# Two blocks of attention layers on one core: scores of two row groups issued in turn into two banks, and weighted sums with the head loop innermost

## The chip, the core and the metric

The kernel runs on one core of a Trainium2 chip. The metric is the time on the device in microseconds (us). Three runs of the kernel before took 1917.32, 1917.56 and 1919.44 us; the median is 1917.56 us.

## The reference, cut to what matters

256 tokens of width 1024 pass two layers of a first block (feed-forward, mixer, feed-forward) and two layers of a second block. The change lies in the mixer of the first block, which has three attentions beside each other; the one it touches most is the forgetting attention, 8 heads of 64 channels:

```python
u = rmsnorm(h); q, k, v = heads(u @ w_in)         # 8 heads of 64, 256 tokens
c = cumsum(log_sigmoid(f_logit + b_forget))       # per head, over the tokens
z = q @ k.T * 64 ** -0.5 + c[:, None] - c[None, :]
o_fx = softmax(where(k_pos <= q_pos, z, -max)) @ v
o_sb = ...    # stick-breaking attention, 8 heads of 64: weights w from a cumulative sum, then w @ v
o_mem = ...   # 4 heads of 128 on a memory of 256 tokens
h = h + rmsnorm((g_sb * (o_sb @ w_sb) + g_fx * (o_fx @ w_fx) + g_mem * (o_mem @ w_mem)) @ w_out)
```

All is float32.

## The kernel before

**Main line and tasks.** TensorE runs strictly in the order in which the program emits it. Its main line is the products with the weights. A weight chunk of 128 x 1024 is loaded (`raw`), cast into a high part by ScalarE (`hi`, L270) and into a rest by VectorE (`lo`, L271), and each product is three matmuls, at L287, L288 and L290 for products with tokens in the rows (tiles `acc`, `gu`), and at L298 to L300 for those with channels in the rows (`mm`, `cf`). Eight `hi` and eight `lo` buffers exist, so a cast of a chunk waits until TensorE has finished the chunk eight places back. What hangs on other engines is emitted by tasks (Python generators). The program keeps a clock `now` of TensorE's work in ns: `tick(ns)` advances it, each product by its own columns, and a task that yields a number of ns (`DELAY`) goes on once `now` has advanced so far. So a smaller tick in a task puts more products of the main line between that task and what follows. The other engines' orders are made by a scheduler.

**The mixer** (`mixer`, L760) runs in this order: projections of queries and keys (`mm`), then the three gates (`acc`, 3 x 8 chunks, each chunk for token tile 0 and then for token tile 1), then three branch products, then the output product. Beside them the tasks put in the three attentions, one after the other.

**Forgetting attention** (`forgetting`, L666). A unit (`forgetting_unit`, L677) takes the scores of a token tile t of 128 queries: at t = 0 four heads with 128 keys each, at t = 1 two heads with 256 keys, so that a unit fills one bank of PSUM. Heads 4e+j lie at partitions 64e to 64e+63 of block j of q and k, so e says which half of the array's rows a head's score product uses, and all heads of a unit have the same e. There are two such banks (`z_bank`, bufs=2), used in turn. A layer has six units: t = 0 with e = 0 and 1, then t = 1 with e = 0 (two), e = 1 (two). A unit's scores (L684) are followed on VectorE by one add of the decay per head (L690) and a row maximum (L547), on ScalarE by one exponential per head (L551), which is the last reader of the bank. Units are `fox_gap` = 2000 ns and the unit's tick of 860 ns apart.

**Weighted sum** (`weighted`, L555): normalize (L560, L561), transpose p into a bank `tr` (L383; two such banks, in turn), copy it out (pT, L564), multiply with v (L570) into another `tr` bank, and split the result into `acth` (ScalarE, L375) and `actl` (VectorE, L376). For heads of 64 channels, head i goes to partitions 64 (i % 2) of the result, which is one half of the array's columns. The loop is head by head, and within a head over its key tiles. `stick_breaking_half` (L586) has the same kind of sum for its heads at L631, and `memory_unit` (L705) uses z banks and `weighted` with heads of 128.

In the page's forms, 64*128 is a matmul on 64 rows and 128 columns of the array, 128*64 one on 128 rows and 64 columns. Each float32 matmul of q, k, p and v is two instructions in the trace, so a unit's 4 matmuls at t = 0 are 8, and its 2 at t = 1 are 4.

Of the kernel before, what the change touches and what calls it, by code (L numbers as in the profile page):

```python
# [29 lines left out]
# ---------------------------------------------------------------- host layout  # L30
def _by_k(w):
    """[K, N] -> [K/128, 128, N]"""
    return w.reshape(w.shape[0] // P, P, w.shape[1])


def _by_col(w):
    """[K, n*128] -> [n, 128, (K/128)*128]: one chunk holds all of K for 128 columns."""
    k, n = w.shape[0] // P, w.shape[1] // P
    return w.reshape(k, P, n, P).transpose(2, 1, 0, 3).reshape(n, P, k * P)


def _side_by_side(parts):
    """[K, w] each -> [K/128, 128, sum of w]"""
    return _by_k(np.concatenate(parts, axis=1))


def _woven(parts):
    """[K, n*128] each -> chunks of 128 columns, in turn from each part"""
    return np.stack([_by_col(p) for p in parts], axis=1).reshape(-1, P, parts[0].shape[0])


def _pairs(a):
    """[n, 128, w] -> [n/2, 128, 2w]"""
    n, p, w = a.shape
    return a.reshape(n // 2, 2, p, w).transpose(0, 2, 1, 3).reshape(n // 2, p, 2 * w)


def _head_cols(w, first, width, stride, n):
    """Columns first..first+width of each of n heads, stride apart."""
# [3 lines left out]
def _halves(w):  # L63
    """Columns of eight heads of 64 in the order 0 4 1 5 2 6 3 7"""
# [10 lines left out]
def _three(w):  # L75
    """[8*128, 320] -> 3 chunks of three row tiles, the last one's third tile being zeros"""
# [20 lines left out]
def _per_partition(I):  # L97
    """Small per-channel vectors, channel c at partition c % 128."""
# [13 lines left out]
def _consts():  # L112
    """Constants of the shapes alone: masks, rotary tables."""
    i = np.arange(P)
    after = (i[:, None] > i[None, :])          # [k, k']: 1 where k > k'
    strict = (i[:, None] < i[None, :])         # [k, q]: 1 where k < q
    cmask = np.where(i[None, :] <= i[:, None], 0.0, NEG)   # [q, k]
# [11 lines left out]
# ---------------------------------------------------------------- program  # L129
class Act:  # L130
    """An operand [nk*128 channels, 256 tokens], channel-major, in a high and a low part; tiles of
    four channel blocks."""
# [12 lines left out]
    def part(self, k, n, t):  # L145
        """Blocks k..k+n of the tokens of tile t, both parts"""
# [12 lines left out]
class Program:  # L159
    """TensorE runs in the order of emission. The products with weights are its main line; what  # L160
    hangs on other engines' results (transposes, attention) is emitted by tasks, generators that
    yield how many ns of TensorE's work are to lie before their next step."""
# [8 lines left out]
                 decay=8000, fox_gap=2000, fox_p=13900, mem_gap=3000, mem_p=19500, mem_norm=17000, conv0=2200, conv_gap=3000,  # L171
# [17 lines left out]
    # -- tasks  # L189
# [44 lines left out]
    # -- tiles  # L234
# [18 lines left out]
    # -- inputs  # L253
# [7 lines left out]
    def take(self, src, i, parts=1):  # L261
        """Chunk i of a re-laid weight, split exactly into a high part and the rest."""
# [18 lines left out]
    # -- matrix products  # L281
    def mm_a(self, outs, x, k, t, hi, lo, first, last):
        """Token-major: outs += x[k, tokens of t].T @ chunk; outs: [(psum, columns of the chunk)]"""
# [9 lines left out]
    def mm_b(self, ps, x, hi, lo, nk, base=0):  # L293
        """Channel-major: ps[128 channels, 256 tokens] = sum over k of chunk[k].T @ x[k]"""
# [8 lines left out]
    def cols_b(self, src, blocks, x, nk, per, evac):  # L303
        """Blocks of 128 channels, `per` of them in a chunk; evac(block, psum [128, 2, 256]) for
        every two blocks."""
# [10 lines left out]
    def rows_a(self, chunks, outs, x, done, head=0, tail=0, ready=(None, None)):  # L316
        """Token-major products over all of K. chunks: functions that give a row tile's chunk;
        outs[t]: the accumulators; done(t) follows the last product of token tile t. The first
        `head` and the last `tail` row tiles go to one token tile after the other, so that what
        comes before or after on the other engines runs beside products; of the last ones, also  # L320
        one accumulator after the other. ready: the tasks that make x for each token tile."""
# [34 lines left out]
    def whole(self, src, nk, per=1, parts=1):  # L356
        """Row tiles, `per` of them in a chunk"""
# [10 lines left out]
    def banks(self, n, w=512):  # L368
        """Accumulators of n row products of width w for both token tiles, and their columns"""
# [3 lines left out]
    def split(self, dst, src, lo_engine=None):  # L373
        """dst[0] + dst[1] = src exactly"""
# [3 lines left out]
    def transposed(self, *parts):  # L378
        """[128, n*128] each -> psum [128, all blocks, 128]"""
# [11 lines left out]
    # -- norms  # L391
    def rstd(self, sums):
        """(sum of sums + eps)^-1/2, sums being shares of a mean of squares"""
# [9 lines left out]
    def mean_sq(self, src, scale):  # L403
        """The row sums of (scale * src)^2"""
# [16 lines left out]
    def gained(self, ps, g):  # L421
        """ps [128 channels, 4 blocks, 128] times the blocks' gains g [128, 4]"""
# [4 lines left out]
    def pre_gain(self, t, g, x, r, delay):  # L427
        """x[:, tokens of t] = h * g, transposed and split; the norm's factor r[:, t] is left to the
        products' results."""
# [12 lines left out]
    def pre_norm(self, t, g, x, delay, h=None):  # L442
        """x[:, tokens of t] = norm of h, transposed and split"""
# [7 lines left out]
    def residual(self, t, ps, post):  # L451
        """h += ps, or its norm with the gain `post`"""
# [15 lines left out]
    def across(self, r, ready):  # L468
        """r [128 tokens, 2] -> [128, 256]: r of every token, for every partition"""
# [22 lines left out]
    def out_proj(self, src, nk, x, post, nxt, tail=None, before={}, head=0, ready=(None, None)):  # L492
        """h += (norm of) x @ w for w [nk*128, 1024]; then what the next phase needs of h, by the
        tasks returned. before: tasks to join before a row tile."""
# [17 lines left out]
    # -- feed-forward of the first block  # L512
    def ffn(self, name, gw, uw, dw, l, x, r, ready, mid, nxt, early=None):
        """x: the norm's input times its gain; r [128, 2]: what its rows are to be scaled by.
        mid(), called halfway, gives the gain of the norm behind."""
# [25 lines left out]
    # -- attention  # L541
    def softmax(self, z, nh, nk, scale):
        """exp(scale * z - its row's maximum) of z [128 q, nh, nk], and the rows' sums"""
# [11 lines left out]
    def weighted(self, kind, p, sums, nh, nk, v, d, dst):  # L555
        """p [128 q, nh, nk] @ v / sums for nh heads of d channels, channel-major and split, into dst;
        v(a, i): values of head i's key tile a"""
# [10 lines left out]
        for i in range(nh):  # L568
            for a in range(nk // P):
                nc.tensor.matmul(ps[d * (i % n):d * (i % n) + d, i // n], v(a, i), pT[:, i, a], start=a == 0, stop=a == nk // P - 1)  # L570
        self.tick(nh * (nk // P) * 215)
        self.split(dst, ps[:, :nh // n])

    def keep_before(self, x, engine):
        """x [128 k, 4 heads, 128 q] where k < q, else 0"""
# [10 lines left out]
    def stick_breaking_half(self, e, q, k, v, x):  # L586
        """Heads 4e+j, at partitions 64e of block j; scores are [k, q]."""
# [40 lines left out]
        for b in range(NT):  # L628
            for j in range(4):
                for a in range(b + 1):  # L630
                    nc.tensor.matmul(ps[64 * (j % 2):64 * (j % 2) + 64, j // 2, b * P:b * P + P],  # L631
                                     v[:, a, (4 * e + j) * 64:(4 * e + j) * 64 + 64], w[a, b][:, j * P:j * P + P],
                                     start=a == 0, stop=a == b)
        self.tick(12 * 215)
        self.split(x.blocks(2 * e, 2), ps)

    def decay(self, f, bias, got):
        """f [8 heads, 256]: c = cumsum(log_sigmoid(f + bias)). Gives c of the queries [128, 8] for
        both tiles, c of the keys for every partition, and the latter with the causal mask taken off."""
# [625 lines left out]
```

## Time and profile before

| | |
|---|---|
| median of three runs | 1917.56 us |
| profiled execution, first to last instruction | 1915.3 us |
| TensorE matmul busy | 1882.2 us (98%) |
| VectorE busy | 1199.0 us (63%) |
| ScalarE busy | 970.8 us (51%) |
| mean granted TensorE clock | 0.995 of 2.4 GHz |
| DMA queue of the weights, share of 16 engines | 53.5% |

The profiled execution is shown by its span; the page gives no separate device time for it, and the median of the runs is 2.3 us longer than the span, which is taken as what lies around it. A row of the timeline gives the start, the time to the end of the last of the merged instructions, engine, line, operation, tiles, form and count; in brackets is the engine's idle time before it and what ended that. Matmuls overlap: the next starts before the one before it has ended, so the distance of starts is the rate.

### The profile page before, as it was taken

The numbers are of one execution on the slowest core, as the hardware profiler recorded it, in microseconds if no ns is written. First come the engines' busy times: TensorE is split into PE (matmuls) and PEld (weight loads), VectorE is DVE, ScalarE is ACT, GpSimd is POOL, SyncE is SP. The second block draws the span as 40 slices with busy tenths as digits, with TensorE's granted clock in tenths as the row PEclk, the third lists the DMA queues.
The fourth block names the chain that finished last, engine by engine and source line by source line (L and its number), as shares of the span: only waits on it lengthen the run. The fifth ranks groups of instructions, "written<-read, shape, count | busy, mean of one in ns | idle before, by whom it ended". The sixth has DMA issues, their size and how long they took to land.

```text
span 1915.3 us, 26948 instructions
## 1 busy us (share of the span) xinstructions
PE 1882.2 (98%) x10390; PEld 1605.8 (84%) x10390; DVE 1199.0 (63%) x1522; ACT 970.8 (51%) x1419; POOL 276.0 (14%) x243
## 2 busy tenths in 40 slices
PE   8999999999999999999999999999999989999988
PEld 6888999778788888889987878888989977889976
DVE  5564756676655465547657765546768756658763
ACT  5454545455544354536545654445456544547552
POOL 1000103102100020001310120001414313103320
PEclk9999999999999999999999999999999999999999
DMA  8456665445555655566553545565655554425551
GB/s 295 178 201 206 222 208 177 143 150 170 197 177 176 198 197 176 176 198 224 184 165 112 187 167 185 189 197 188 189 192 178 176 177 151 154 99 182 181 178 65
DMA packets 95344, 343.08 MB, mean 179 GB/s; under 512 B 10720, under 2 KB 10992, under 8 KB 95216
## 3 DMA queue, kind: packets, MB, share of 16 engines
q1 hardware_dynamic: 95216, 341.37, 53.5%
q8 instruction: 81, 1.33, 0.3%
q14 instruction: 47, 0.39, 0.1%
HBM read 339.21 MB, written 2.11 MB: 178 GB/s over the span
## 4 chain that ended last, share of the span: by engine, by line
PE 89%; DVE 4%; POOL 2%; ACT 2%; issue 2%; DMA 1%; DVEq 0%; SPq 0%; POOLq 0%; ACTq 0%
PE acc L287 12%; PE acc L288 12%; PE acc L290 12%; PE gu L288 8%; PE gu L290 8%; PE gu L287 8%; PE tr L383 3%; PE mm L298 3%; PE mm L299 3%; PE mm L300 3%; PE cf L299 2%; PE cf L300 2%; PE cf L298 2%; DVE lo L271 2%; ACT hi L270 1%
## 5 line engine op out<-in xcount | busy, mean ns | idle before, releaser
L271 DVE TENSOR_TENSOR lo<-raw,hi 128x1024 fp32r<-128x1024 f32 (+3 forms) x616 | 760.4, 1242 | 316.5 <-ACT hi L270 313.2
L270 ACT CAST hi<-raw 128x1024 fp32r<-128x1024 f32 (+3 forms) x616 | 640.2, 1043 | 360.5 <-PE acc L290 196.9
L287 PE MATMUL acc<-hi,acth 128*128 128x512 f32 x1072 | 433.3, 404 | 10.9 <-DVE cgu L966 10.9
L288 PE MATMUL acc<-lo,acth 128*128 128x512 f32 x1072 | 424.9, 396 | 0.0
L290 PE MATMUL acc<-hi,actl 128*128 128x512 f32 x1072 | 347.2, 396 | 0.0
L287 PE MATMUL gu<-hi,acth 128*128 128x512 f32 x704 | 281.2, 399 | 0.0
L288 PE MATMUL gu<-lo,acth 128*128 128x512 f32 x704 | 278.5, 396 | 0.2 <-DVE lo L271 0.2
L287 PEld LDWEIGHTS acc<-hi,acth 128*128 128x128 f32 x1072 | 202.8, 189 | 61.2 <-DVE cgu L966 12.2
L290 PEld LDWEIGHTS acc<-hi,actl 128*128 128x128 f32 x1072 | 202.5, 189 | 48.2 <-DVE actl L376 0.5
L288 PEld LDWEIGHTS acc<-lo,acth 128*128 128x128 f32 x1072 | 203.0, 189 | 43.9
L290 PE MATMUL gu<-hi,actl 128*128 128x512 f32 x704 | 226.1, 395 | 0.0
L400 POOL TENSOR_TENSOR r<-v,mhalf 128x1 f32<-128x1 f32 x40 | 50.7, 1267 | 943.8 <-DVE v L397 935.1
L298 PE MATMUL cf<-acth,hi 128*128 128x256 f32 x576 | 162.2, 282 | 0.0
L300 PE MATMUL cf<-acth,lo 128*128 128x256 f32 x576 | 161.9, 281 | 0.0
L299 PE MATMUL cf<-actl,hi 128*128 128x256 f32 x576 | 161.8, 281 | 0.0
L290 PEld LDWEIGHTS gu<-hi,actl 128*128 128x128 f32 x704 | 132.5, 188 | 31.0
L288 PEld LDWEIGHTS gu<-lo,acth 128*128 128x128 f32 x704 | 132.7, 188 | 30.3 <-DVE lo L271 0.9
L287 PEld LDWEIGHTS gu<-hi,acth 128*128 128x128 f32 x704 | 132.7, 189 | 28.8
L376 DVE TENSOR_TENSOR actl<-tr,acth 128x512 fp32r<-128x512 f32 (+2 forms) x126 | 75.1, 607 | 108.1 <-ACT acth L375 108.0
L375 ACT CAST acth<-tr 128x512 fp32r<-128x512 f32 (+2 forms) x126 | 64.2, 520 | 144.1 <-PE tr L383 111.4
L298 PE MATMUL mm<-acth,hi 128*128 128x256 f32 x432 | 123.2, 285 | 0.0
L300 PE MATMUL mm<-acth,lo 128*128 128x256 f32 x432 | 121.4, 281 | 0.0
(234 smaller groups left out, 2387.8 us busy)
## 6 DMA issues: line engine op xcount, KB each, us to landing
raw<-ffn_gu SPq DMA_DIRECT2D x175, 512.0 KB, 4.9
raw<-ffn_dn SPq DMA_DIRECT2D x88, 512.0 KB, 4.3
raw<-cf_up SPq DMA_DIRECT2D x88, 512.0 KB, 3.6
raw<-gate SPq DMA_DIRECT2D x48, 512.0 KB, 3.6
raw<-cf_dn SPq DMA_DIRECT2D x44, 512.0 KB, 3.6
raw<-a_in SPq DMA_DIRECT2D x18, 512.0 KB, 5.0
gain<-gains SPq DMA_DIRECT2D x17, 512.0 KB, 4.9
raw<-in_v SPq DMA_DIRECT2D x16, 516.0 KB, 3.6
```

What stands on the lines that cost most here:

```text
L270: self.last_hi = nc.scalar.copy(out=hi[:, cs], in_=raw[:, cs])
L271: nc.vector.tensor_tensor(out=lo[:, cs], in0=raw[:, cs], in1=hi[:, cs].bitcast(F32), op=ALU.subtract)
L287: nc.tensor.matmul(ps, x.h(k, ts), hi[:, cs], start=first, stop=False)
L288: nc.tensor.matmul(ps, x.h(k, ts), lo[:, cs], start=False, stop=False)
L290: nc.tensor.matmul(ps, x.l(k, ts), hi[:, cs], start=False, stop=last)
L298: nc.tensor.matmul(ps, hi[:, c], x.h(k), start=k == 0, stop=False)
L299: nc.tensor.matmul(ps, hi[:, c], x.l(k), start=False, stop=False)
L300: nc.tensor.matmul(ps, lo[:, c], x.h(k), start=False, stop=k == nk - 1)
L375: self.nc.scalar.copy(out=dst[0], in_=src)
L376: (lo_engine or self.nc.vector).tensor_tensor(out=dst[1], in0=src, in1=dst[0].bitcast(F32), op=ALU.subtract)
L383: self.nc.tensor.transpose(ps[:, w * P:w * P + P], n[:, c * P:c * P + P], self.ident)
L400: nc.gpsimd.tensor_tensor(out=r, in0=v, in1=self.mhalf, op=ALU.pow)
```

## The change

Scores of a pair of units, e = 0 and e = 1, are now emitted together (`forgetting_scores`): both z banks are taken, and the matmuls alternate between heads j and 4+j. Two units per pair then go on with a bank each, the second spawned `fox_e` = 300 ns later. A layer has three pairs (t = 0; t = 1 with j 0 and 1; t = 1 with j 2 and 3), `fox_gap` = 4600 ns and a tick of 900 ns apart. In the weighted sums of heads of 64, two heads alternate innermost, and their ticks are halved. For heads of 128 (n = 1) the loop and the tick are as before. The comments and docstrings are blanked, which changes no instruction.

```diff
-                 decay=8000, fox_gap=2000, fox_p=13900, ...
+                 decay=8000, fox_gap=4600, fox_e=300, fox_p=13900, ...
@@ weighted
-        for i in range(nh):
+        for i0 in range(0, nh, n):
             for a in range(nk // P):
-                nc.tensor.matmul(ps[d * (i % n):d * (i % n) + d, i // n], v(a, i), pT[:, i, a], start=a == 0, stop=a == nk // P - 1)
-        self.tick(nh * (nk // P) * 215)
+                for i in range(i0, i0 + n):
+                    nc.tensor.matmul(ps[d * (i % n):d * (i % n) + d, i // n], v(a, i), pT[:, i, a], start=a == 0, stop=a == nk // P - 1)
+        self.tick(nh * (nk // P) * 215 // n)
@@ stick_breaking_half
-            for j in range(4):
-                for a in range(b + 1):
-                    nc.tensor.matmul(...)
-        self.tick(12 * 215)
+            for j, a in [(j0 + j, a) for j0 in (0, 2) for a in range(b + 1) for j in range(2)]:
+                nc.tensor.matmul(...)
+        self.tick(6 * 215)
@@ forgetting
-            for e in range(2):
-                for j0 in range(0, 4, nh):
-                    tasks.append(self.spawn(self.forgetting_unit(t, e, j0, nh, q, k, v, decay, x)))
-                    yield self.DELAY["fox_gap"]
+            for j0 in range(0, 4, nh):
+                zs = self.forgetting_scores(t, j0, nh, q, k)
+                for e in range(2):
+                    tasks.append(self.spawn(self.forgetting_unit(zs[e], t, e, j0, nh, v, decay, x), self.DELAY["fox_e"] * e))
+                yield self.DELAY["fox_gap"]
+    def forgetting_scores(self, t, j0, nh, q, k):
+        n = (t + 1) * P
+        zs = [self.z_bank().rearrange("p (h k) -> p h k", k=n) for _ in range(2)]
+        for i in range(nh):
+            for e in range(2):
+                rows = slice(64 * e, 64 * e + 64)
+                self.nc.tensor.matmul(zs[e][:, i], q[rows, j0 + i, t * P:t * P + P], k[rows, j0 + i, :n], start=True, stop=True)
+        self.tick(900)
+        return zs
```

**Scores on TensorE**, first layer, the units of t = 1 before (`z_3444` and `z_3467` are the two banks; `acc` are products of a gate; the words in brackets are the engines whose semaphores the instruction waits for):

```order
L290 MATMUL acc01_3323<-hi_3433,actl_149 128x512
L684 MATMUL z_3444<-kf_2792,qf_2634 128x256 [waits DVE_49,Activation_49]
L684 MATMUL z_3444<-kf_2792,qf_2634 128x256
L287 MATMUL acc00_3322<-hi_3456,acth_147 128x512
L288 MATMUL acc00_3322<-lo_3457,acth_147 128x512
L287 MATMUL acc01_3323<-hi_3456,acth_147 128x512
L288 MATMUL acc01_3323<-lo_3457,acth_147 128x512
L290 MATMUL acc00_3322<-hi_3456,actl_149 128x512
L290 MATMUL acc01_3323<-hi_3456,actl_149 128x512
L684 MATMUL z_3467<-kf_2792,qf_2634 128x256 [waits DVE_49,Activation_49]
L684 MATMUL z_3467<-kf_2792,qf_2634 128x256
```

The same place in the change, the second pair (`z_3470` and `z_3471` are the two banks):

```order
L290 MATMUL acc11_3310<-hi_3324,actl_148 128x512
L685 MATMUL z_3470<-kf_2792,qf_2634 128x256 [waits DVE_49,Activation_49]
L685 MATMUL z_3471<-kf_2792,qf_2634 128x256 [waits DVE_49,Activation_49]
L685 MATMUL z_3470<-kf_2792,qf_2634 128x256
L685 MATMUL z_3471<-kf_2792,qf_2634 128x256
L287 MATMUL acc10_3309<-hi_3351,acth_146 128x512
```

Before, six products lie between two units, and each waits for one bank. Now 18 products lie between two pairs, and a pair waits for both banks, in a row, with the products queued behind.

**VectorE beside them**, first layer, before:

```order
L690 SCALAR_TENSOR_TENSOR z<-z,cq,c_2504 128x128 x4
L547 TENSOR_REDUCE m<-z 128x4
L690 SCALAR_TENSOR_TENSOR z<-z,cq,c_2504 128x128 x4
L547 TENSOR_REDUCE m<-z 128x4
L690 SCALAR_TENSOR_TENSOR z<-z,cq,ck 128x256 x2
L547 TENSOR_REDUCE m<-z 128x2
L832 SCALAR_TENSOR_TENSOR gate<-acc_3322,rows,bias 128x512
L690 SCALAR_TENSOR_TENSOR z<-z,cq,ck 128x256
```

and in the change:

```order
L697 SCALAR_TENSOR_TENSOR z<-z,cq,c_2504 128x128 x8
L547 TENSOR_REDUCE m<-z 128x4
L839 SCALAR_TENSOR_TENSOR gate<-acc_3307,rows,bias 128x512
L547 TENSOR_REDUCE m<-z 128x4
L839 SCALAR_TENSOR_TENSOR gate<-acc_3308,rows,bias 128x512
L271 TENSOR_TENSOR lo<-raw,hi 128x1024 x2
L697 SCALAR_TENSOR_TENSOR z<-z,cq,ck 128x256 x4
L547 TENSOR_REDUCE m<-z 128x2
L271 TENSOR_TENSOR lo<-raw,hi 128x1024
L547 TENSOR_REDUCE m<-z 128x2
L271 TENSOR_TENSOR lo<-raw,hi 128x1024 x2
L697 SCALAR_TENSOR_TENSOR z<-z,cq,ck 128x256 x4
```

The adds of both banks of a pair now come first, alternating, then the two maxima with a gate's evacuation between them (in the later pairs a cast `lo`). On ScalarE a cast `hi` now stands before the pair's eight exponentials, three casts between the first and the second pair's, and one between the two banks of the second pair.

**Weighted sums on TensorE**, first layer, the first units' before:

```order
L570 MATMUL tr<-pT,vf 64x128 x4
L383 MATMUL tr<-ident,p 128x128 x4
L287 MATMUL acc_3570<-hi,acth 128x512
L288 MATMUL acc_3570<-lo,acth 128x512
L287 MATMUL acc_3571<-hi,acth 128x512
L288 MATMUL acc_3571<-lo,acth 128x512
L290 MATMUL acc_3570<-hi,actl 128x512
L290 MATMUL acc_3571<-hi,actl 128x512
L570 MATMUL tr<-pT,vf 64x128 x4
```

and in the change:

```order
L571 MATMUL tr<-pT,vf 64x128 x4
L383 MATMUL tr<-ident,p 128x128 x4
L571 MATMUL tr<-pT,vf 64x128 x4
L383 MATMUL tr<-ident,p 128x128 x4
L287 MATMUL acc_3554<-hi,acth 128x512
```

The six products between the first and the second unit's weighted sum are gone, and the same holds for the third and fourth unit. With two `tr` banks in turn, the second sum goes into the bank of the first. The halved ticks also put the second stick-breaking half 12 matmuls of the main line later, put the third and fourth memory unit's scores, and their weighted sums, in a row without products between, and leave all else of TensorE's order as it was. The second layer has the same moves.

## Rows read from the trace of the kernel before

**Rows 1.** The page: busy time of the engines over the span, and the granted TensorE clock in 40 slices, in tenths.

```profile
PE 1882.2 (98%) x10390; PEld 1605.8 (84%) x10390; DVE 1199.0 (63%) x1522; ACT 970.8 (51%) x1419; POOL 276.0 (14%) x243
PEclk9999999999999999999999999999999999999999
```

**Rows 2.** The waits of TensorE's matmuls over the whole run, longest in total first: who waited for whom, us in total, times, longest.

```profile
PE acc L287 <- DVE cgu L966: 10.9, 3, 5.2
...
PE tr L383 <- DVE nrm L435: 3.3, 2, 2.0
...
PE tr L383 <- POOL gate L859: 1.8, 2, 0.9
```

**Rows 3.** The timeline of TensorE around the first layer's units of scores (start, us, engine, line).

```profile
371.75 0.40 PE L287 MATMUL acc<-hi,acth 128*128 128x512 f32 x1
...
373.15 0.40 PE L287 MATMUL acc<-hi,acth 128*128 128x512 f32 x1
...
374.64 1.16 PE L684 MATMUL z<-kf,qf 64*128 64x128 f32 x8
375.73 0.50 PE L287 MATMUL acc<-hi,acth 128*128 128x512 f32 x1
...
377.33 1.16 PE L684 MATMUL z<-kf,qf 64*128 64x128 f32 x8
378.42 0.51 PE L287 MATMUL acc<-hi,acth 128*128 128x512 f32 x1
...
380.03 1.13 PE L684 MATMUL z<-kf,qf 64*128 64x256 f32 x4
381.09 0.50 PE L287 MATMUL acc<-hi,acth 128*128 128x512 f32 x1
...
383.73 0.50 PE L287 MATMUL acc<-hi,acth 128*128 128x512 f32 x1
```

**Rows 4.** The timeline of TensorE at the first unit's weighted sum (t = 0) and at the third's (t = 1).

```profile
401.22 0.66 PE L570 MATMUL tr<-pT,vf 128*64 128x128 f32 x8
401.81 0.66 PE L383 MATMUL tr<-ident,p 128*128 128x128 f32 x4
402.22 0.48 PE L287 MATMUL acc<-hi,acth 128*128 128x512 f32 x1
...
406.36 0.66 PE L570 MATMUL tr<-pT,vf 128*64 128x128 f32 x8
```

**Rows 5.** The timeline of VectorE beside the units of scores.

```profile
375.84 1.54 DVE L690 SCALAR_TENSOR_TENSOR z<-z,cq,c 128x128 f32<-128x128 f32 x4 [5.53 <-PE z L684]
377.41 0.69 DVE L547 TENSOR_REDUCE m<-z 128x4 f32<-128x512 f32 x1
...
381.26 1.02 DVE L690 SCALAR_TENSOR_TENSOR z<-z,cq,ck 128x256 f32<-128x256 f32 x2 [0.47 <-PE z L684]
382.32 0.69 DVE L547 TENSOR_REDUCE m<-z 128x2 f32<-128x512 f32 x1
382.93 0.74 DVE L832 SCALAR_TENSOR_TENSOR gate<-acc,rows,bias 128x512 f32<-128x512 f32 x1
...
386.96 1.22 DVE L271 TENSOR_TENSOR lo<-raw,hi 128x1024 fp32r<-128x1024 f32 x1
```

**Rows 6.** The timeline of ScalarE beside the units of scores: the first and the last exponential of the first unit, the two of the third, and a cast.

```profile
378.14 0.37 ACT L551 ACTIVATE p<-z,m 128x128 f32<-128x128 f32 x1 [9.96 <-DVE m L547]
...
379.18 0.37 ACT L551 ACTIVATE p<-z,m 128x128 f32<-128x128 f32 x1
...
383.11 0.47 ACT L551 ACTIVATE p<-z,m 128x256 f32<-128x256 f32 x1 [0.70 <-DVE m L547]
...
383.57 0.47 ACT L551 ACTIVATE p<-z,m 128x256 f32<-128x256 f32 x1
...
385.47 1.04 ACT L270 CAST hi<-raw 128x1024 fp32r<-128x1024 f32 x1 [1.34 <-issue]
```

**Rows 7.** The timeline of ScalarE at the first unit's weighted sum.

```profile
401.93 0.37 ACT L375 CAST acth<-tr 128x256 fp32r<-128x256 f32 x1 [1.42 <-PE tr L570]
402.50 0.59 ACT L564 COPY pT<-tr 128x512 f32<-128x512 f32 x1 [0.20 <-PE tr L383]
```

**Rows 8.** The timeline of VectorE there.

```profile
402.59 0.42 DVE L376 TENSOR_TENSOR actl<-tr,acth 128x256 fp32r<-128x256 f32 x1
```

**Rows 9.** The timeline of TensorE after three of its idle stretches (the idle time is in brackets), and two products 1 and 2 us after the third.

```profile
505.12 1.23 PE L383 MATMUL tr<-ident,nrm 128*128 128x128 f32 x8 [1.27 <-DVE nrm L435]
...
1134.47 1.23 PE L383 MATMUL tr<-ident,nrm 128*128 128x128 f32 x8 [2.04 <-DVE nrm L435]
...
1624.45 0.30 PE L383 MATMUL tr<-ident,kr 128*128 128x128 f32 x1 [1.96 <-DVE kr L1013]
...
1625.29 0.59 PE L287 MATMUL acc<-hi,acth 128*128 128x512 f32 x1
...
1626.53 0.63 PE L287 MATMUL acc<-hi,acth 128*128 128x512 f32 x1
```

**Rows 10.** Stretches after those idle times: busy time of each engine (count), granted clock, DMA share, GB/s.

```profile
1625.40:1628.70 3.30, 3.30 (x10) 2.52 (x9) 1.92 (x6) 0.78 (x2) 0.76 (x3) 0.50 0.46 166
1132.40:1137.40 5.00, 2.96 (x17) 2.42 (x17) 3.95 (x8) 2.62 (x6) 1.58 (x3) 1.00 0.73 274
503.80:508.80 5.00, 3.73 (x21) 3.04 (x21) 3.20 (x6) 2.62 (x6) 1.02 (x3) 1.00 0.75 265
```

More of the change, by code (lines that the diff above doesn't have):

```diff
@@ L170 @@
                  fox_pT=3600, att_pT=3600, lat_pT=3600, sb_half=34600, sb_z=2600, sb_ln=6100, sb_cum=2000, sb_w=3000,
[L171 removed]
+                 decay=8000, fox_gap=4600, fox_e=300, fox_p=13900, mem_gap=3000, mem_p=19500, mem_norm=17000, conv0=2200, conv_gap=3000,
                  cf_gap=4100, kv=6700, q=2600, rope=5600, lat_gap=2200, lat_p=9000, n_conv=4000, n_ffnA=1500,
@@ L628, in stick_breaking_half @@
         for b in range(NT):
-            for j in range(4):
-                for a in range(b + 1):
-                    nc.tensor.matmul(ps[64 * (j % 2):64 * (j % 2) + 64, j // 2, b * P:b * P + P],
-                                     v[:, a, (4 * e + j) * 64:(4 * e + j) * 64 + 64], w[a, b][:, j * P:j * P + P],
-                                     start=a == 0, stop=a == b)
-        self.tick(12 * 215)
+            for j, a in [(j0 + j, a) for j0 in (0, 2) for a in range(b + 1) for j in range(2)]:
+                nc.tensor.matmul(ps[64 * (j % 2):64 * (j % 2) + 64, j // 2, b * P:b * P + P],
+                                 v[:, a, (4 * e + j) * 64:(4 * e + j) * 64 + 64], w[a, b][:, j * P:j * P + P],
+                                 start=a == 0, stop=a == b)
+        self.tick(6 * 215)
         self.split(x.blocks(2 * e, 2), ps)
@@ L670, in forgetting, with forgetting_unit @@
             nh = 4 // (t + 1)
-            for e in range(2):
-                for j0 in range(0, 4, nh):
-                    tasks.append(self.spawn(self.forgetting_unit(t, e, j0, nh, q, k, v, decay, x)))
-                    yield self.DELAY["fox_gap"]
-        yield from self.wait(*tasks)
-    def forgetting_unit(self, t, e, j0, nh, q, k, v, decay, x):
+            for j0 in range(0, 4, nh):
[3 more added lines that the diff above has]
+                yield self.DELAY["fox_gap"]
+        yield from self.wait(*tasks)
+    def forgetting_scores(self, t, j0, nh, q, k):
+        n = (t + 1) * P
+        zs = [self.z_bank().rearrange("p (h k) -> p h k", k=n) for _ in range(2)]
+        for i in range(nh):
+            for e in range(2):
+                rows = slice(64 * e, 64 * e + 64)
+                self.nc.tensor.matmul(zs[e][:, i], q[rows, j0 + i, t * P:t * P + P], k[rows, j0 + i, :n], start=True, stop=True)
+        self.tick(900)
+        return zs
+    def forgetting_unit(self, z, t, e, j0, nh, v, decay, x):
         nc = self.nc
@@ L680, in forgetting_unit @@
         n = (t + 1) * P
-        rows = slice(64 * e, 64 * e + 64)
-        z = self.z_bank().rearrange("p (h k) -> p h k", k=n)
-        for i in range(nh):
-            nc.tensor.matmul(z[:, i], q[rows, j0 + i, t * P:t * P + P], k[rows, j0 + i, :n], start=True, stop=True)
-        self.tick(860)
         h0 = 4 * e + j0
```

## The prediction

> **What bounds the kernel.** I read the page first. TensorE is busy for 98% of the span at the full clock, VectorE for 63% and ScalarE for 51% [rows 1], so time is won by taking work off TensorE and lost by letting it wait. The waits of TensorE come next: the longest are at phase ends in other parts (10.9 us before the second block's down products), and of the mixer the list has only 1.8 us before the transposes of the merged gates. No score (L684) and no weighted sum (L570, L631) stands in it [rows 2]. So in the mixer TensorE runs without a hole, and a term of this change counts in full. Then the timeline of TensorE around the scores shows what a unit costs, and those of VectorE and ScalarE show how long a bank is held.
>
> **What the change takes off: entries, exits, and half of the score time.** Six products of the gate take 373.15 - 371.75 = 1.40 us. With a unit of t = 0 between, it is 378.42 - 375.73 = 2.69 us, so the unit costs 1.29 us; one of t = 1 costs 383.73 - 381.09 - 1.40 = 1.24 us [rows 3]. The unit's own eight instructions span 1.16 us (four of t = 1: 1.13), the rest is entry and exit. If the two halves of the array's rows work at once, a pair costs one unit instead of two, and a layer saves 1.29 + 2 x 1.24 = 3.77 us, two layers **7.5 us**. No row shows two halves of rows (64\*128) with different heads in a row. The nearest shows halves of columns (128\*64): eight instructions of 128 columns span 0.66 us there [rows 4] and 1.16 us in a unit, which uses one half alone [rows 3]. So halves of the array do run at once in the one direction, and I take it that they do in the other. If they don't, a pair saves only 1.29 - 1.16 = 0.13 us, or 1.24 - 1.13 = 0.11 us, 0.7 us in two layers. Bounds: 0.7 to 7.5 us saved.
>
> The Trainium skill, "TensorEngine Tiling (Array Packing)", section "Key Properties", has tiles at different positions execute in parallel, rows as well as columns. By it the saving is the 7.5 us, by the nearest rows of the same direction it is the 0.7 us; no run here shows which.
>
> **The head loop in the weighted sums: nothing.** At t = 0 a head has one key tile, so the old order already alternates the column halves; at t = 1 it doesn't, two key tiles of a head follow each other. Both span the same 0.66 us [rows 4]. So the order within a sum doesn't matter, and the new order for t = 1 and for stick-breaking is put at 0, between -0.3 and +0.3 us in all. The halved ticks cost nothing by themselves; what they move is below. Later stick-breaking scores keep their neighbours: 0.
>
> **What it adds: the second bank of a pair comes free late.** TensorE waits in order, so a pair's first products wait for both banks of the pair before, and 18 gate products are queued behind. I count from the first score of the first pair.
> - TensorE is back at the gate after 375.73 - 374.64 = 1.09 us, then 18 products take 1.60 + 2 x 1.40 us (the first six with the unit's exit and entry, 375.73 to 377.33): it arrives at the second pair at 5.5 us [rows 3].
> - VectorE starts its adds 375.84 - 374.64 = 1.20 us after the first score. Four take 377.41 - 375.84 = 1.57 us, and all eight now come first: 4.34 us. The first maximum (0.69) ends at 5.0 us; with the gate's evacuation in between (steps of 0.61 and 0.7 us) the second ends at 6.3 us [rows 5].
> - ScalarE needs 379.18 + 0.37 - 378.14 = 1.41 us for a bank's four exponentials [rows 6]. The first bank's run from 5.1 to 6.5 us, the second's to 7.9 us; the cast that now stands before them adds 0.1.
> So the second bank is free at 8.0 us, and TensorE waits **2.5 us**. Without the evacuation and the cast it would still be 2.4, since the exponentials of both banks follow each other. Before, one bank was served in 379.55 - 374.64 = 4.9 us and asked for again only after two units, 380.03 - 374.64 = 5.4 us.
>
> The third pair: TensorE is back at the gate at 8.0 + 1.06 = 9.1 us and arrives at 13.5 us. VectorE has two casts `lo` before its adds, the second of which needs a `hi` that ScalarE makes after the exponentials, to 9.0 us; so it ends at about 10.2 us (1.22 each). Four adds (1.02 for two) end at 12.2, the first maximum at 12.9, another cast, the second maximum at 14.6 us [rows 5]. ScalarE makes casts of 1.04 us that wait for gate products behind the second pair, at 13.2 us the first bank's exponentials (0.47 each), then a cast, then the second's, to 16.1 us [rows 6]. A wait of **2.7 us**. Without any cast between it would be 9.2 + 2.0 + 0.7 + 2 x 0.95 = 13.9 us, a wait of 0.4. I take 2.7, since the casts do stand there in the engines' orders. Per layer 5.2 us, in two layers **10.4 us**; bounds 2 x (2.4 + 0.4) = 5.6 and, with a cast more on either wait, 12.5 us.
>
> The Trainium skill, "Perfetto Trace Analysis", section "Matmuls", wants independent groups to rotate through PSUM banks so that the emptying of one lies beside the next one's matmuls. The old order does that, the new one takes both banks at once. By the rule alone the whole service of a pair would lie open, 8.0 - 1.1 = 6.9 us; by the rows the 18 products cover all but 2.5.
>
> **Weighted sums in a row.** The second sum needs the bank of the first. After the first sum starts, the transposes start at 0.59 us and take 0.41 [rows 4], so the second wants to start at about 1.1 us. The first is cast from 0.71 to 1.08 us [rows 7], and the rest takes 0.42 [rows 8]: free at 1.5 us. 0.4 us, twice a layer, **1.6 us** in all; bounds 0 and, if a cast `lo` goes first, 1.6 + 4 x 0.6 = 4 us. The memory units: the fourth's scores follow the third's without a product between and need the second's bank, and its weighted sum follows a transpose whose copy takes 0.59 us [rows 7]. 0.1 and 0.2 us a layer, **0.6 us**; bounds 0 and 2 (a cast of ScalarE ahead of each).
>
> **The clock.** After idle times of 1.27 and 2.04 us the granted clock stayed at 1.00, 2.4 GHz; after one of 1.96 us it fell to 0.50, 1.2 GHz, for some 3.3 us [rows 9, 10], in which three products took 1626.53 - 1625.29 = 1.24 us instead of 0.70 [rows 3, 9]: 1.5 us lost. The new waits are broken by the first bank's scores, into pieces of 1 to 2 us. I take one fall in the four long waits, **1.5 us**; bounds 0 and 6.
>
> **The sum**, against the profiled execution: 1915.3 - 7.5 + 10.4 + 1.6 + 0.6 + 1.5 = 1921.9 us. With the 2.3 us by which the median is longer, 1924.2 us, 0.34% above 1917.56.
>
> **Rivals.**
> - *Shorter waits*: the casts find a gap and both banks are served at their floor, 5.6 us in two layers, and the clock holds: -7.5 + 5.6 + 1.6 + 0.6 = +0.3, **1917.9 us**. For it: VectorE has idle time in this place (0.47 us before the third unit's adds). Against it: the orders above are fixed.
> - *Both banks free in time* (faster): place, the second and third pair; the row halves work at once and no pair waits: -7.5 + 1.6 + 0.6 = -5.3, **1912.3 us**. It decides below 1.5 us of waits at the pairs in two layers, since then the time is less by 0.2% (3.8 us, about what a measurement of this kernel tells from no change). For it speaks only that adds in alternating banks might not have to follow each other; but four are busy for 1.54 us of their 1.57 [rows 5], so little is to be had, and 18 products would have to last 7 us instead of 4.4.
> - *Row halves one after the other*: -0.7 + 10.4 + 1.6 + 0.6 + 1.5 = +13.4, **1931.0 us**. For it: no row shows row halves at once. Against: column halves do.
> - *Nothing that can be told*: the interleaving does not reach TensorE as written, or gain and waits cancel by chance, **1917.6 us**.
>
> **Chances.** Forecast 0.55, its own range 1920 to 1929 (waits 8 to 12.5, none to three falls of the clock). Shorter waits 0.17, in time 0.10, one after the other 0.13, nothing 0.05. Faster by over 0.2% (under 1913.7): 0.10 and 0.03 of the shorter waits, 0.13. Slower (over 1921.4): 0.50 of the forecast and 0.13, so 0.63. Within 0.2%: 0.24. A range from 1915.5 to 1931.5 leaves out the rival in time (0.10), half of the one with serial halves (0.06) and the forecast's ends (0.04).
>
> **What would show it.** Right: sixteen score instructions of a pair in about the 1.16 us of one unit now; two waits per layer of TensorE at the scores for ScalarE's exponentials, of 2 to 3 us in total each; small ones at the weighted sums for `actl`; weighted sums still at 0.66 us. Wrong in the gain if a pair spans over 2 us; wrong in the waits if the list of TensorE's waits has no score; wrong on the clock if it stays at 1.00 through the mixer or falls at each wait.

## The result, and the profile after

The changed kernel takes 1929.07 us (median of 4 runs, 1925.11 to 1930.72) against 1917.56 us, a ratio of 1.0058 (95% interval 1.0046 to 1.007): slower by 0.6%, 4.9 us above the forecast and inside its range of 1915.5 to 1931.5. Its profiled execution spans 1928.9 us, 13.6 more than before. The page's first line shows the same instructions on every engine, and TensorE still at 98% [rows 1]:

```profile
PE 1885.6 (98%) x10390; PEld 1608.1 (83%) x10390; DVE 1196.8 (62%) x1522; ACT 967.9 (50%) x1419; POOL 277.2 (14%) x243
```

The list of TensorE's waits has rows now that were not in [rows 2]: the scores (L685) behind ScalarE's exponentials, and the weighted sums (L571). The wait for `nrm` grew from 3.3 to 4.2 us.

```profile
PE acc L287 <- DVE cgu L973: 10.9, 3, 5.2
PE z L685 <- ACT p L551: 7.5, 8, 1.2
PE tr L383 <- DVE nrm L435: 4.2, 2, 2.5
...
PE tr L571 <- ACT pT L564: 1.5, 2, 0.7
...
PE tr L571 <- DVE actl L376: 0.7, 2, 0.3
```

TensorE's timeline at the first layer's three pairs, the counterpart of [rows 3] (start, us, engine, line; the idle time ahead is in brackets):

```profile
376.92 1.16 PE L685 MATMUL z<-kf,qf 64*128 64x128 f32 x16
378.01 0.50 PE L287 MATMUL acc<-hi,acth 128*128 128x512 f32 x1
...
383.64 0.70 PE L685 MATMUL z<-kf,qf 64*128 64x256 f32 x2 [1.20 <-ACT p L551]
385.04 1.13 PE L685 MATMUL z<-kf,qf 64*128 64x256 f32 x6 [0.70 <-ACT p L551]
386.10 0.80 PE L287 MATMUL acc<-hi,acth 128*128 128x512 f32 x1
...
388.82 0.63 PE L287 MATMUL acc<-hi,acth 128*128 128x512 f32 x1
...
392.77 0.70 PE L685 MATMUL z<-kf,qf 64*128 64x256 f32 x2 [0.70 <-ACT p L551]
394.63 1.13 PE L685 MATMUL z<-kf,qf 64*128 64x256 f32 x6 [1.16 <-ACT p L551]
395.68 0.50 PE L287 MATMUL acc<-hi,acth 128*128 128x512 f32 x1
```

Sixteen score instructions take the 1.16 us of eight before. Each later pair waits twice: 1.20 us for the first bank, then, after the two instructions that fit, 0.70 us for the second. Behind the second pair the products take 0.63 us instead of 0.39: the clock has fallen. Its stretches (the last three columns are granted clock, DMA share, GB/s), all at 1.00 before:

```profile
385.00:390.00 5.00, 4.96 (x16) 3.82 (x17) 3.39 (x6) 1.81 (x2) 0.00 (x0) 0.66 0.62 196
395.00:400.00 5.00, 5.00 (x18) 3.73 (x15) 3.64 (x7) 1.78 (x5) 0.00 (x0) 0.66 0.86 283
510.00:515.00 5.00, 3.42 (x13) 2.86 (x14) 3.54 (x7) 2.62 (x6) 1.04 (x3) 0.73 0.72 241
1030.00:1035.00 5.00, 4.95 (x16) 3.80 (x17) 3.27 (x7) 0.89 (x2) 0.00 (x0) 0.66 0.81 287
1145.00:1150.00 5.00, 2.49 (x12) 2.17 (x11) 3.84 (x8) 2.29 (x6) 0.73 (x2) 0.72 0.74 233
```

Five falls to 0.50 (1.2 GHz), three behind pairs and two behind the wait for `nrm`. VectorE and then ScalarE beside the first pair show what a pair's service consists of (counterparts of [rows 5, 6]):

```profile
378.11 2.17 DVE L697 SCALAR_TENSOR_TENSOR z<-z,cq,c 128x128 f32<-128x128 f32 x8 [6.22 <-PE z L685]
380.19 0.68 DVE L547 TENSOR_REDUCE m<-z 128x4 f32<-128x512 f32 x1
380.79 0.74 DVE L839 SCALAR_TENSOR_TENSOR gate<-acc,rows,bias 128x512 f32<-128x512 f32 x1
381.44 0.68 DVE L547 TENSOR_REDUCE m<-z 128x4 f32<-128x512 f32 x1
```

```profile
381.14 1.05 ACT L270 CAST hi<-raw 128x1024 fp32r<-128x1024 f32 x1 [10.67 <-PE acc L290]
382.09 0.36 ACT L551 ACTIVATE p<-z,m 128x128 f32<-128x128 f32 x1
...
383.47 0.38 ACT L551 ACTIVATE p<-z,m 128x128 f32<-128x128 f32 x1
...
384.50 0.40 ACT L551 ACTIVATE p<-z,m 128x128 f32<-128x128 f32 x1
```

The gate's evacuation (L839) lies between the two maxima and a cast ahead of the eight exponentials; the last one ends 384.50 + 0.40 = 384.90, 8.0 us after the first score. For the second pair VectorE's second maximum and ScalarE's casts stand like this:

```profile
391.33 0.68 DVE L547 TENSOR_REDUCE m<-z 128x2 f32<-128x512 f32 x1
```

```profile
390.75 1.05 ACT L270 CAST hi<-raw 128x1024 fp32r<-128x1024 f32 x1 [0.60 <-PE acc L290]
...
392.61 1.04 ACT L270 CAST hi<-raw 128x1024 fp32r<-128x1024 f32 x1
```

**Where the time went**, summed over TensorE's timeline of both layers. An interruption of the products costs the time from the start of the last product ahead to the start of the first one behind, less the 0.23 us of a product:

| | before | after | change | forecast |
|---|---|---|---|---|
| scores | 13.9 | 17.6 | +3.7 | -7.5 + 10.4 |
| weighted sums, their transposes, memory scores | 28.3 | 33.2 | +4.9 | +2.2 |
| transposes of the gates and of `nrm` (with the waits for `nrm`) | 12.6 | 14.4 | +1.8 | 0 |
| products themselves (mostly the clock) | | | +4.5 | +1.5 |
| the rest of the kernel | | | -0.9 | 0 |

The rows add up to 14.0, the spans to 13.6. The +4.5 is a balance: by the trace the products of the two mixers last about 6 us longer in the five falls, and 15 fewer interruptions, each of which delays the product behind it by another 0.1 us, give 1.5 us back.

One of the twelve runs of e9 below, the profiled one, had a mean granted clock of 0.557 and took 3079 us; it is left out, and so no trace of e9 is read.

### The profile page after: what moved, and what is told of

The parts are those of the page before. It is cut to its first block, busy times and chain, and to the rows that moved or that the text cites. A ratio compares the mean times of both kernels' runs of the same rounds, so it can differ in the third digit from the quotient of the medians.

```text
span 1928.9 us, 26956 instructions
## 1 busy us (share of the span) xinstructions
PE 1885.6 (98%) x10390; PEld 1608.1 (83%) x10390; DVE 1196.8 (62%) x1522; ACT 967.9 (50%) x1419; POOL 277.2 (14%) x243
## 5 line engine op out<-in xcount | busy, mean ns | idle before, releaser
L299 PE MATMUL mm<-actl,hi 128*128 128x256 f32 x432 | 121.4, 281 | 0.0
```

The lines of the kernel that those rows point to most:

```text
L299: nc.tensor.matmul(ps, hi[:, c], x.l(k), start=False, stop=False)
```

## Experiments

Between them the medians of before lie from 1916.8 to 1917.5 us; each ratio is against the runs of before beside it.

### The loops alone (e1_loops)

The kernel before, with the new order inside the weighted sums (here that of L570; the stick-breaking sums likewise) and the old ticks.

```
-        for i in range(nh):
+        for i0 in range(0, nh, n):
             for a in range(nk // P):
-                nc.tensor.matmul(ps[d * (i % n):...
+                for i in range(i0, i0 + n):
+                    nc.tensor.matmul(ps[d * (i % n):...
```

> The kernel before with the two new inner loop orders alone; ticks, delays and scores as before. Theory (the column halves already work at once in either order): no change, 1917.6 us within 1 us, and the weighted sums of t = 1 stay at eight instructions in 0.66 us. Rival (the order is worth something, and the change gained there what it lost at the scores): 1915 us or less.

1917.98 us, ratio 1.0003 (0.9994 to 1.0012). The loop order is worth nothing, as put.

### Bank after bank (e2_bank_by_bank)

The changed kernel with the two score loops exchanged.

```
-        for i in range(nh):
-            for e in range(2):
+        for e in range(2):
+            for i in range(nh):
```

> The changed kernel, but of a pair all scores of e = 0 are issued before those of e = 1. Theory (TensorE goes ahead to the other half of the rows as it does with columns, so turn-taking is not needed): a pair still spans 1.2 to 1.4 us and the time stays at 1925 to 1931 us. Rival (only issue in turn lets the halves overlap): a pair spans about 2.1 us, 0.9 us more per pair, 6 pairs, up to 5 us more: 1930 to 1936 us, less what the waits give back.

1920.1 us, ratio 1.0018 (1.0009 to 1.0027): the theory missed in span and time, and the rival had the cause right (only issue in turn lets the halves overlap) but not the time. TensorE's timeline:

```profile
377.62 1.71 PE L685 MATMUL z<-kf,qf 64*128 64x128 f32 x16
...
383.61 1.13 PE L685 MATMUL z<-kf,qf 64*128 64x256 f32 x4
385.26 1.13 PE L685 MATMUL z<-kf,qf 64*128 64x256 f32 x4 [0.52 <-ACT p L551]
...
390.69 2.37 PE L685 MATMUL z<-kf,qf 64*128 64x256 f32 x8
```

The row halves run beside each other only where the program alternates them: eight instructions of t = 1 take 2.37 us here (0.11 of it idle), 1.13 where a pair that alternates does not wait (e7, below). So the gain is gone (all scores cost 13.8 us, as before the change), but so are the waits (1.0 us in two layers), since TensorE fills the first bank while the second is still served. e2 keeps the halved ticks and the 18 products and is still 9.0 us faster than the changed kernel, so the loss also hangs on both banks being asked for in turn.

### More products between the pairs (e3_gap30, e4_gap30_room)

The changed kernel with 30 products between pairs instead of 18; then also the old loops and ticks, and sums due 8 us after their scores.

```
-  fox_gap=4600, fox_e=300, fox_p=13900
+  fox_gap=7200, fox_e=300, fox_p=13900    (e3)
+  fox_gap=7200, fox_e=300, fox_p=8000     (e4, with loops and ticks as before)
```

> The changed kernel with fox_gap 7200 instead of 4600 ns: 30 gate products between pairs instead of 18, so TensorE arrives at a pair about 8.3 us after the pair before. The four memory units' scores then stand in a row at the gates' end. Theory (a bank is held about 8 us because two units are served together): the waits at the pairs fall from 2 us of idle time per wait to under 0.5 us, and no fall of the clock follows them: -8 to -13 us there; the memory scores in a row bring two new waits of 2 to 3 us per layer: about 1922 us (1916 to 1927). Rival (the wait comes from something else than the distance, as casts that go with it): the waits at the pairs stay over 1.5 us each and the time at 1929 or above.

> Paired scores with fox_gap 7200 and fox_p 8000 (13900), weighted sums in the old loop order and with the old ticks, so that the second stick-breaking half and the memory units stand as before. Theory: the pairs' gain stays whole and its waits are gone: 1917.6 - 7.5 + 1 to 2 us of small waits at the weighted sums = 1911 to 1913 us, the granted clock at 1.00 through the mixer. Rival (the wait moves to the transposes, whose normalized weights now are due 5.9 us of products earlier): waits of the same size before L383 of p, 1917 us or more.

1924.1 us, ratio 1.0033 (1.0021 to 1.0045), and 1913.73, ratio 0.9983 (0.9975 to 0.9992). e3 is inside its theory's range, e4 just above. In both no score waits at the pairs; a pair of t = 1 is all eight instructions in 1.13 us at once. In e3 the next work is late instead, the transposes and the memory scores:

```profile
PE tr L383 <- DVE p L561: 3.6, 2, 1.8
PE z L716 <- DVE lo L271: 3.5, 2, 1.8
...
PE z L716 <- ACT p L551: 1.6, 2, 0.8
```

Two falls of the clock stand behind e3's memory scores. In e4 only 3.1 us for `p` are left of these. But e4 changes the gap, the time of the sums and the ticks in one, so the next runs take them apart.

### The paired scores alone (e5_scores_only)

The changed kernel with loops and ticks of the sums as before; the gap stays at 18 products.

```
-        self.tick(nh * (nk // P) * 215 // n)
+        self.tick(nh * (nk // P) * 215)
...
-        self.tick(6 * 215)
+        self.tick(12 * 215)
```

> Only the paired scores with their gap of 18 products; loops and ticks of the weighted sums as before. In the order of TensorE the four sums still lie in two rows as in the changed kernel, and only the memory units keep their old places. Theory (the pairing alone makes the loss): waits at the scores for exponentials 7 to 8 us in two layers, waits at the sums about 2 us, 16 score instructions in 1.16 us; time 1924 to 1930 us. Rival (the halved ticks make a good part of it, by what they move toward the next feed-forward): below 1923 us, and the wait for nrm back at 3.3 us.

1914.48 us, ratio 0.9987 (0.9978 to 0.9996): the theory fell, and what it held of the pairing with it. The scores wait 1.4 us in two layers, not 7.5:

```profile
374.99 1.16 PE L685 MATMUL z<-kf,qf 64*128 64x128 f32 x16
...
380.54 0.70 PE L685 MATMUL z<-kf,qf 64*128 64x256 f32 x2
381.94 1.13 PE L685 MATMUL z<-kf,qf 64*128 64x256 f32 x6 [0.70 <-ACT p L551]
...
387.36 1.44 PE L685 MATMUL z<-kf,qf 64*128 64x256 f32 x8
```

VectorE has both maxima in a row and the gate's evacuations behind them:

```profile
376.19 2.17 DVE L697 SCALAR_TENSOR_TENSOR z<-z,cq,c 128x128 f32<-128x128 f32 x8 [5.53 <-PE z L685]
378.27 1.28 DVE L547 TENSOR_REDUCE m<-z 128x4 f32<-128x512 f32 x2
380.35 1.41 DVE L839 SCALAR_TENSOR_TENSOR gate<-acc,rows,bias 128x512 f32<-128x512 f32 x2 [0.80 <-PE acc L290]
```

ScalarE's first and last exponential of this pair:

```profile
378.98 0.37 ACT L551 ACTIVATE p<-z,m 128x128 f32<-128x128 f32 x1 [10.45 <-DVE m L547]
...
381.39 0.40 ACT L551 ACTIVATE p<-z,m 128x128 f32<-128x128 f32 x1
```

So the exponentials start 378.98 - 374.99 = 4.0 us after the first score instead of 5.2, and the last one ends after 6.8 us instead of 8.0. TensorE comes to the second pair at 380.54 and gets its second bank at 381.94, 1.40 us later. The scores lie 12 products earlier in the gate: the halved tick behind the stick-breaking sums (L634) had moved them. The text of the change has the halved ticks leave the rest of TensorE's order as it was; that was wrong, for all scores of the forgetting attention come 12 products later too.

### 24 products (e6_gap24) and the sums later (e7_gap30_late)

As e5, with other numbers:

```
-  fox_gap=4600, fox_e=300, fox_p=13900
+  fox_gap=6000, fox_e=300, fox_p=9000     (e6)
+  fox_gap=7200, fox_e=300, fox_p=10500    (e7)
```

> Paired scores with 24 products between pairs, loops and ticks of the sums as before, the sums due 9 us after their scores. Theory (the wait is what 18 products, 4.4 us, do not cover of a service of 7 us): six products more cover 1.40 us of each of the four waits of 2.6, so about 1.2 us stays at each, 5 us in two layers, and the clock falls less often; time 1915 to 1920 us. Rival (the bank is held longer when more products need their casts): waits stay above 2 us each and the time at 1922 or more.

> Paired scores with 30 products between pairs as in the run before, the sums due 10.5 us after their scores instead of 8. Theory (what is left there is TensorE waiting 1.5 us per layer for the scaled weights p before the first transposes): that wait is gone, 3.1 us off 1913.7, so 1909 to 1912 us. Rival (two sums with six products between now wait for their bank, as in the changed kernel): waits at L570 or L383 of 1 to 2 us per layer, 1913 to 1915 us.

e6: 1915.1 us, ratio 0.999 (0.9981 to 0.9998). The time is in the theory's range, but not by its sum: the scores wait only 1.1 us (the service here is 7 us, not 8), and the transposes between sums in a row wait 4.0 us for `actl`. e7: 1908.4 us, ratio 0.9956 (0.9943 to 0.9968), the fastest version and a little below its theory's range. Nothing of pairs, sums or memory stands in its list of waits; the scores cost 8.1 us (before 13.9), and two sums in a row with no transposes between share one entry and exit, 16 instructions in 1.09 us where one sum with its transposes kept the products off for 402.22 - 401.22 = 1.00 [rows 4]:

```profile
391.40 1.13 PE L685 MATMUL z<-kf,qf 64*128 64x256 f32 x8
...
397.79 1.09 PE L570 MATMUL tr<-pT,vf 128*64 128x128 f32 x16
```

### Work laid into the waits (e8_fill)

```
         zs = [self.z_bank()... for _ in range(2)]
+        if t:
+            fill = self.tr_bank()
+            for w in range(12):
+                self.nc.tensor.transpose(fill[:, w % 4 * P:w % 4 * P + P], self.ident, self.ident)
```

> The changed kernel with 12 transposes of the identity, whose result nobody reads, ahead of the scores of the second and third pair: work of about 1.85 us laid into each of the four waits, which are 2.6 us long. Theory (the clock falls because TensorE idles there): the scores start and end when they did, no fall of the granted clock follows the pairs, three times 1.5 us come back: 1923 to 1926 us. Rival (the clock falls there for another reason, or its fall costs little): 1928 to 1931 us. If the transposes do not fit into the waits the time rises over 1931.

1922.39 us, ratio 1.0025 (1.0015 to 1.0034): 6.7 us less than the changed kernel and just below the theory's range, although TensorE does more. The scores come at the same distance from the products (1.47 us of transposes in the place of 1.20 of waiting):

```profile
384.18 1.47 PE L685 MATMUL tr<-ident 128*128 128x128 f32 x12
385.58 0.70 PE L689 MATMUL z<-kf,qf 64*128 64x256 f32 x2
386.95 1.13 PE L689 MATMUL z<-kf,qf 64*128 64x256 f32 x6 [0.67 <-ACT p L551]
```

and no stretch of the two mixers, from 365 to 560 and from 980 to 1200 us, has a granted clock under 1.00; two of those shown above:

```profile
385.00:390.00 5.00, 4.33 (x23) 3.02 (x22) 2.96 (x5) 3.09 (x14) 0.00 (x0) 1.00 0.32 108
...
1145.00:1150.00 5.00, 5.00 (x23) 4.06 (x22) 2.40 (x3) 4.21 (x5) 0.90 (x1) 1.00 0.07 27
```

Not all of the 6.7 us is shown to be the clock's: the wait for `nrm`, where nothing was laid in, is 2.0 us shorter than in the changed kernel (2.2 against 4.2).

### The place in the gate (e9_sb_tick, e10_late_scores, e11_ticks_only, e12_gap30_12on)

One tick decides the place. e9 gives it back to the changed kernel, e10 and e12 take it from e5 and e7, and e11 halves both ticks in the kernel of e1, where nothing is paired.

```
-        self.tick(6 * 215)
+        self.tick(12 * 215)     (e9; e10, e11 and e12 the other way)
```

> The changed kernel with one number back: the tick behind the stick-breaking sums is 12*215 again, which puts the scores 12 products earlier in the gate, to the place where they lie in the run with the paired scores alone (the gate's evacuation behind both maxima, no cast ahead of the exponentials). Theory (the wait at the pairs is set by what VectorE and ScalarE are given between the two banks, and that by the place of the scores in the gate): waits at the scores 1 to 2 us in two layers instead of 7.5, no fall of the clock behind them, 1914 to 1918 us. Rival (the halved ticks of the forgetting sums or the new loops make the loss): 1924 us or more.

> The opposite: paired scores, loops and ticks of the forgetting sums as before, only the tick behind the stick-breaking sums halved, so that the scores lie 12 products later, as in the changed kernel (a gate evacuation between the two maxima). Theory: the waits of 7 to 8 us at the scores come back and the falls of the clock with them, 1923 to 1930 us. Rival (the place of the scores is not it): 1918 us or less.

> The kernel before with the new loops and both ticks halved, scores unit by unit as before but 12 products later. Theory (the later place costs only where both banks are asked for at once; a unit asks for the bank of two units ago): waits at the scores under 2 us in two layers, 1915 to 1920 us. Rival (the halved ticks cost whatever the scores do): 1922 us or more.

> The paired scores with 30 products between pairs and the sums due after 10.5 us (1908.4 us), with the tick behind the stick-breaking sums halved, so that the scores lie 12 products later, with the gate's evacuation between the two maxima, as in the changed kernel. Theory (a place is dear only where the products between two requests do not cover the service it makes; 30 products last 7 us and the longest service seen was 8.0): at most 0.5 us of wait at each pair, under 1 us in two layers; the third and fourth memory units now follow each other without a product between and may wait 1 to 2.6 us per layer; 1909 to 1915 us. Rival (the later place costs its 11 to 14 us whatever lies between the pairs): 1919 us or more.

| scores | old place | 12 products later |
|---|---|---|
| unit by unit | before 1917.56; e1 1917.98 | e11 1928.01, ratio 1.0058 (1.0045 to 1.007) |
| in pairs, 18 products | e5 1914.48; e9 1915.79, ratio 0.9995 (0.9986 to 1.0004) | changed 1929.07; e10 1928.78, ratio 1.0064 (1.0051 to 1.0077) |
| in pairs, 30 products, sums after 10.5 us | e7 1908.4 | e12 1916.42, ratio 0.9998 (0.9989 to 1.0007) |

One number takes 13.3 us off the changed kernel (e9; whether its waits went as the theory had it was not seen). e10 is the case with a trace, and its waits and falls are those of the changed kernel; all four of its pairs with waits are followed by a fall:

```profile
PE z L685 <- ACT p L551: 7.6, 8, 1.2
```

For e11 the theory missed: the later place costs 10 us against e1 without any pairing. In each layer a unit waits 2.10 us, and in the second the clock falls behind it:

```profile
1020.39 1.72 PE L684 MATMUL z<-kf,qf 64*128 64x256 f32 x4 [2.10 <-ACT p L551]
```

```profile
1020.00:1025.00 5.00, 4.61 (x11) 2.81 (x11) 2.84 (x5) 1.25 (x6) 0.00 (x0) 0.58 0.69 211
1025.00:1030.00 5.00, 5.00 (x11) 3.54 (x12) 2.02 (x3) 2.06 (x6) 0.00 (x0) 0.50 0.11 17
```

In e12 the pairs do not wait in the later place either, as the theory had it; 1916.42 is above its range and 8 us above e7. In its profiled execution (1920.09 us, above the median) the second sum now waits 2.3 us a layer for its copy `pT`, and the clock falls behind that wait in both layers; the first:

```profile
404.13 0.66 PE L570 MATMUL tr<-pT,vf 128*64 128x128 f32 x8 [2.34 <-ACT pT L564]
```

## Why the prediction was right in its sign and wrong in its cause

- **Saved scores**: right. A pair interrupts the products for 1.16 to 1.19 us where two units took 2.3; 6.9 us in two layers and, with six re-entries of 0.1 us fewer, 7.5, as forecast. The rival of serial row halves is out, with a condition that the text did not have: the halves must alternate in the program (e2). Its price was wrong too: it kept 10.4 us of waits beside serial halves, 1931.0 us, and e2, the nearest case, idles 1.0 us at the scores and takes 1920.1. The Trainium skill, "TensorEngine Tiling (Array Packing)", section "Key Properties", says that tiles can execute in parallel; the alternating order agrees (16 instructions in 1.16 us), the order bank after bank does not show it at t = 1 (8 in 2.37).
- **Loop order**: nothing, as put (e1).
- **Waits at the pairs**: the size was right, 2.66 + 2.62 us a layer (a pair's interruption less that of an undisturbed one) against 2.5 + 2.7, partly by luck, and what they were put down to was wrong. The step that failed is the floor of the first wait: "Without the evacuation and the cast it would still be 2.4, since the exponentials of both banks follow each other". In e5, without them, it is 1.4. Two errors had cancelled in the 2.5: eight adds in alternating banks take 2.17 us, not twice 1.57, and the cast ahead of the exponentials cost 382.09 - 380.87 = 1.2 us, not 0.1. At the third pair the mechanism held: without a cast between, the text put 0.4, and in e5 a pair's interruption is only 0.3 us longer there than that of an undisturbed one. But the casts do not come with the pairing: they come from the place of the scores, and that from the halved ticks, of which the text said that they "cost nothing by themselves; what they move is below". What they moved was priced, but as a cost of the pairing. The rival "shorter waits" was held down to 0.17 because "the orders above are fixed"; they are fixed by one tick.
- **A rival that was missing**: that the ticks alone make a loss. They do: e11 has no pairs and is 10 us slower than e1, by another wait (one unit a layer, 2.1 us) and a long fall of the clock. How much the late place costs depends on how the banks are asked for: 10 us unit by unit, 13 to 14 in pairs that alternate; and e2, in the late place with bank after bank, ends only 0.2% above the kernel before.
- **Weighted sums and memory units**: right in kind, too small: 2.2 forecast, 4.9 measured. Of the sums in a row one waits 0.34 us for `actl`, but the other 0.73 for the copy `pT`, which was not in the text; the memory units' scores and sums that now stand in a row cost 1.0 us a layer more, where 0.3 was put.
- **The clock**: one fall of 1.5 us forecast, five came, about 6 us. With the sums (2.7 more than put) and the longer wait for `nrm` that is most of what is missing between the forecast 6.6 and the measured 13.6 us. For the three falls behind pairs e8 shows that it is the idling: with work in the waits they are gone. The two behind `nrm` are gone there too, but so is half of that wait, and e1, with neither pairs nor new ticks, has such a fall as well, behind a wait of 2.25 us for `nrm` (granted clock 0.66 from 1135 to 1140 us); that they come from the change is not shown. "Falls at each wait" was named as what would show the term wrong.
- **The covering products**: the Trainium skill, "Perfetto Trace Analysis", section "Matmuls", wants groups to rotate through banks so that emptying one lies beside the next one's matmuls. By that alone the 6.9 us of service would lie open; 2.6 did at 18 products in the late place, 1.4 and 0.3 in the early one, nothing at 30.

No run moves one of the moved instructions alone, but the traces tell which of them was waited for at the first layer's pairs. In the changed kernel the first maximum of the first pair is done at 380.19 + 0.68 = 380.87, 3.95 us after the first score, and ScalarE starts the exponentials only behind its cast, after 5.17; in e5, without the cast, it starts them after 3.99. From there both kernels need 2.81 us. The second maximum was done at 381.44 + 0.68 = 382.12, before ScalarE came to the second bank at 383.47, so the gate's evacuation between the maxima cost nothing there. At the second pair the second maximum was done at 391.33 + 0.68 = 392.01, and ScalarE came to the second bank only behind a cast from 392.61 to 393.65. So it is ScalarE's casts `hi` that held the banks. Why a later place brings them in front of the exponentials is not shown. That halved ticks in the forgetting sums add nothing in e11 was not run by itself either; e9 and e5, between which they and the loops lie, differ by 1.3 us, and their ratios' intervals overlap.

## What to carry to other kernels

A number that only paces a schedule is a change of its own: run it without the rest before its moves are priced as a cost of what it came with, for here it turned a gain of 3 us into a loss of 11. Where a pair of banks is taken at once, put as much work between two requests as the longest service lasts, and look for what is late next (sums, copies) before calling it done. A forecast whose sum comes out right has not shown its terms: here two errors of 1 us cancelled in the very wait on which it rested.

## What the hardware showed beyond that

- Row halves of the array run together when the program alternates them (16 instructions of 128 columns in 1.16 us) and one after the other when it does not (eight of 256 columns in 2.37 us, 0.11 of it idle); at 128 columns a partial overlap is left, 16 in 1.71 us.
- VectorE's adds in place into PSUM are faster when two banks alternate: eight in 2.17 us, against four in 1.54 in one bank.
- Idle pieces of 1.2 and 0.7 us, with two score instructions between them, were followed by a granted clock of 0.50 at three of the four pairs of the changed kernel and at all four of e10; one of 0.70 us alone (e5, twice) was not. The length alone does not decide it: of e11's two idle pieces of 2.10 us one was followed by a fall and one was not.
